# Block 2's four joints: the order of its small mixers, the rooms of the S5 and RG-LRU rows, of the first feed-forward sums and of the raw places

## The chip, the cores and the metric

The kernel runs on one NeuronCore of a Trainium2 chip, in one launch. A core has five engines with their own instruction queues: TensorE (PE; PEld is its weight load), VectorE (DVE), ScalarE (ACT), GpSimd (POOL) and SyncE (SP), which here only issues transfers. Transfers run on 16 DMA engines; SP, ACT and POOL issue them, and a "q" behind an engine's name in the profile is its queue. SBUF is the working memory, PSUM takes what TensorE computes, DRAM tensors carry what doesn't fit. The metric is the device time of one execution in microseconds (us), as the median of several runs.

## The reference

Two transformer blocks run one after the other over 1024 rows of 1024 numbers in fp32: a first one with attention and a mixture of experts, and a second one, cut here to what the change touches.

```python
def second_block(x, ...):
    h = rmsnorm(x, attn_norm[l])
    q, k, v, g, gk_low, s5_u, rg_x, rg_gate = jnp.split(h @ w_in[l], splits, axis=-1)
    y_gla = gla_mixer(q, k, v, g, gk_low, gla_w_gk_up[l], gla_b_gk[l], gla_norm[l])
    y_s5 = rmsnorm(s5_mixer(s5_u, ...), s5_norm[l])
    y_rg = rmsnorm(rglru_mixer(rg_x, rg_gate, ...), rg_norm[l])
    x = x + jnp.concatenate([y_gla, y_s5, y_rg], axis=-1) @ w_out[l]
    h = rmsnorm(x, mlp_norm[l])
    x = x + conv_ffn(h, w_up[l], mlp_conv_w[l], mlp_conv_b[l], w_down[l])
    return rmsnorm(x, final_norm)

def rglru_mixer(xr, gate, ...):
    xc = causal_dwconv(xr, conv_w, conv_b)
    r = jax.nn.sigmoid(jnp.einsum('blhi,hij->blhj', xh, w_a).reshape(B, L, RG_WIDTH) + b_a)
    i = jax.nn.sigmoid(jnp.einsum('blhi,hij->blhj', xh, w_x).reshape(B, L, RG_WIDTH) + b_x)
    log_a = -RG_C * r.astype(f32) * jax.nn.softplus(-lam.astype(f32))
    a = jnp.exp(log_a)
    xin = jnp.sqrt(-jnp.expm1(2.0 * log_a)) * (i * xc).astype(f32)
    _, h = lax.associative_scan(linear_rec_combine, (a, xin), axis=1)
    return h.astype(xr.dtype) * jax.nn.gelu(gate)

def s5_mixer(u, ...):
    ...
    y = jax.nn.gelu(y)
    y = y * jax.nn.sigmoid(y @ w_glu + b_glu)

def conv_ffn(h, w_up, conv_w, conv_b, w_down):
    up, gv = jnp.split(h @ w_up, 2, axis=-1)
    up = causal_dwconv(up, conv_w, conv_b)
    return (jax.nn.gelu(up) * gv) @ w_down
```

The sigmoids are computed as tanh of half the argument, and 1 + tanh is folded into the products that follow.

## The kernel before

Every large product is made of two parts of each factor: a cast to a rounded fp32 form (names with h or hi) and the rest (l or lo); three matmuls of 128x512 take the place of one (lines 260 to 262). The casts are mostly ScalarE's, the subtractions that give the rest VectorE's or GpSimd's. Weights come through a pool of raw tiles (wraw) and of hi and lo tiles (whi, wlo), which is also the room that the change takes for other things.

The second block passes through these stages; each is written once in Python, and a scheduler of the Tile layer sets the order of the instructions on each engine, the waits and the places of the tiles. Pools are opened and closed as stacks: a tile of a new pool lies where an earlier one was, and waits for its last users.

`mix_small` computes S5's input and its states by a scan over the rows (`s5_scan`, VectorE and GpSimd), RG-LRU's convolution (`rg_input`: xc), the two gates' matmuls (prg) with their tanh, the chain of exp, tanh and square root on ScalarE and products and a scan on VectorE, and stores the result, yS[2 + i]. Then comes the S5 output: sixteen groups of three matmuls (py), for which GpSimd copies the factors F (lines 1547 to 1550), VectorE evicts (line 1555), ScalarE applies the activation and issues 32 stores to y_d (line 1558). Then GLA's low-rank part (`gla_low`: pgl, gl), its decays (`gla_decays`: pgk, gz, ge, a scan to gb) and its projections (`gla_qk`: pp, qo), with S5's gate (pglu) between.

`gla_out` runs GLA in eight quads of two turns each (`quad`: decays gx, scores sc, kv, po, the transposes pty and the copies go), and puts the output projection between them. `rest(j)` is the S5 and RG-LRU half of the projection of 128 rows: it loads the raw rows from yS, casts them (YH), subtracts (YL), squares and sums for the norm (pr), makes four products and adds them to x, which it stores to x3_d. `last(j)` adds GLA's half, normalises the rows, and `cols` transposes them (pt) and makes from them the operands of the feed-forward part: 11, 21, 22 and the four differences T1 to T4 of a block product that takes seven half-size products for eight.

The feed-forward part (`Up`) has 22 features. Each loads two weight tiles (wr), makes four block sums on GpSimd (`sums` and `sum4`: fS and in place), casts and splits them (`weights`: wh, wl) and makes seven products (pa, pb, pc). For feature 0 only weights(0, 0) is made ahead; `first` makes its products with 11 and 21, and `first_out`, after the output work pool (ow, "o2work") has closed, makes its sums and other weights:

```python
        s_ow.close()
        self.F.rooms(self.pool(self.fws, "fw2"))
        self.F.first_out()
```

`ffn_down` multiplies the activations (act_d, stored by SP and GpSimd) by the down weights, 77 units of 128x1024 loaded as wraw from act_d and from the weights; `piece` loads a sixteenth of the residual x (res) with every second unit.

The functions that the change touches stand here with the lines of the profile.

Of the kernel before, what the change touches and what calls it, by code (L numbers as in the profile page):

```python
# [186 lines left out]
class K:  # L187
# [1232 lines left out]
    def mix_small(self, ps, st, XH, XL):  # L1420
# [74 lines left out]
        wr = rg.tile([128, 2, 2, 128], F32, name="rgw")  # L1495
        nc.sync.dma_start(wr, a["rg_w"])
        G = []
        for i in range(2):
            G.append([rg.tile([128, 1024], F32, tag=f"rgg{m}", name="rgg", bufs=2) for m in range(2)])
            for m in range(2):  # L1500
                for n in range(2):
                    c = slice(512 * n, 512 * n + 512)
                    pz = ps.tile([128, 512], F32, tag="mm", name="prg", bufs=2)
                    nc.tensor.matmul(pz, wr[:, m, i], xc[i][:, c], start=True, stop=True)
                    nc.scalar.activation(G[i][m][:, c], pz, AF.Tanh, bias=hba[:, m, i:i + 1], scale=0.5)


        for i in range(2):
            t, g = G[i]
            V.scalar_tensor_tensor(xc[i], g, 1.0, xc[i], op0=OP.add, op1=OP.mult)  # L1510
            nc.scalar.activation(g, t, AF.Exp, bias=p2[:, i:i + 1], scale=p2[:, i:i + 1])
        for i in range(2):
            t = G[i][0]
            nc.scalar.activation(t, t, AF.Tanh, bias=p[:, i:i + 1], scale=p[:, i:i + 1])
        for i in range(2):
            t, h = G[i][0], XR[i][:, 0:1024]
            nc.scalar.activation(h, t, AF.Sqrt, scale=0.25)
        for i in range(2):
            t, g = G[i]
            h = XR[i][:, 0:1024]  # L1520
            V.scalar_tensor_tensor(h, g, 1.0, h, op0=OP.add, op1=OP.mult)
            V.tensor_tensor(xc[i], xc[i], h, op=OP.mult)
            V.scalar_tensor_tensor(t, g, 1.0, t, op0=OP.add, op1=OP.mult)
            V.tensor_scalar(t, t, -1.0, 1.0, op0=OP.mult, op1=OP.add)
            V.tensor_tensor_scan(out=h, data0=t, data1=xc[i], initial=0.0, op0=OP.mult, op1=OP.add)
            V.tensor_tensor(xc[i], h, GT[i], op=OP.mult)
            nc.gpsimd.dma_start(self.yS[2 + i], xc[i])

# [32 lines left out]
        self.gla_decays(ps, qk, 0, gl, gu, gb, cm)  # L1561
        for t in range(2):
            self.gla_qk(ps, qk, XH, XL, 0, t)
# [129 lines left out]
    def gla_out(self, ps, lw, ms, XH, XL):  # L1693
# [128 lines left out]
        def rest(j):  # L1822

            c = slice(128 * j, 128 * j + 128)
            raw = ow.tile([128, 4, 128], F32, tag="yr", name="yr", bufs=4)
# [3 lines left out]
            YH, YL = yhl()  # L1829
# [29 lines left out]
        def last(j):  # L1859
# [11 lines left out]
            self.norm_rows(x, gm, xn, s)  # L1871
            if j:
                cols(X.pop(), j - 1)
# [8 lines left out]
        def cols(xn, j):  # L1882
# [81 lines left out]
        self.F.rooms(self.pool(self.fws, "fw2"))  # L1964
# [143 lines left out]
class Up:  # L2108
# [4 lines left out]
    def __init__(self, k):  # L2113
        self.k, self.nc, self.a, self.early, self.wk = k, k.nc, k.a, k.fw, None
        self.R, self.W, self.U, self.A, self.n = {}, {}, {}, {}, {}

    def ring(self, tag, of, dtype=F32):

        n = self.n[tag] = self.n.get(tag, -1) + 1
        first = tag == "wr" and n % of < 2 or n % of == 0  # L2120
        return (self.early if first else self.wk).tile([128, 1024], dtype, tag=f"{tag}{n % of}", name=tag, bufs=1)

    def rooms(self, pool):

        self.wk = pool

        def place(tag, n, dtype=F32):
            self.wk.tile([128, 1024], dtype, tag=tag, name="place", bufs=n)
        for tag, n in (("gv", 2), ("ft", 2), ("fX", 2), ("wr2", 1), ("wr3", 1), ("fS", 1)):
            place(tag, n)  # L2130
        for i in range(1, 5):
            place(f"wh{i}", 1, F32R)
            place(f"wl{i}", 1, F32R)
        self.cv = self.wk.tile([128, 4, 22], F32, name="fcv")
        self.nc.sync.dma_start(self.cv, self.a["fconv"])
# [16 lines left out]
    def sums(self, i):  # L2152

        if i < 22:
            G, t0, t1 = self.nc.gpsimd, self.T0, self.T1
            ru, rv = self.R[i]
            s = self.R[i, "s"] = self.wk.tile([128, 1024], F32, tag="fS", name="fS", bufs=1)
# [27 lines left out]
    def gelu(self, i):  # L2185
# [3 lines left out]
        t = self.A[i] = self.wk.tile([128, 1024], F32, tag="ft", name="ft", bufs=2)  # L2189
# [5 lines left out]
    def pair(self):  # L2195
        return [self.wk.tile([128, 1024], F32, tag="fX", name="fX", bufs=2) for _ in range(2)]
# [130 lines left out]
```

## Time and profile before

| | us |
|---|---|
| median of 3 runs (lowest, highest) | 2086.76 (2086.03, 2090.46) |
| the profiled execution | 2082.21 |
| its span in the profile | 2079.9 |
| TensorE busy | 1919.3 (92%) |
| VectorE busy | 1319.6 (63%) |
| ScalarE busy | 931.4 (45%) |
| GpSimd busy | 721.9 (35%) |
| second block's part of the span, from 1137 on, TensorE's waits in it of over 8 us | 12.8, 10.6 and 8.4 |

The busy time of an engine is an average over stages, so the share of 92% says that most stages are TensorE's and not that all are. The rows further down are from the same profiled execution: a stretch that is cut out with each engine's busy time, the waits of an engine with what released it, and timelines, in which a row may stand for several instructions in a row (x8) and the bracket tells how long the engine had been idle and what it had waited for. Names are those of the program without their buffer numbers.

### The profile page before, as it was taken

The numbers are of one execution on the slowest core, as the hardware profiler recorded it, in microseconds if no ns is written. First come the engines' busy times: TensorE is split into PE (matmuls) and PEld (weight loads), VectorE is DVE, ScalarE is ACT, GpSimd is POOL, SyncE is SP. The second block draws the span as 40 slices with busy tenths as digits, with TensorE's granted clock in tenths as the row PEclk, the third lists the DMA queues.
The fourth block names the chain that finished last, engine by engine and source line by source line (L and its number), as shares of the span: only waits on it lengthen the run. The fifth ranks groups of instructions, "written<-read, shape, count | busy, mean of one in ns | idle before, by whom it ended". The sixth has DMA issues, their size and how long they took to land.

```text
span 2079.9 us, 27638 instructions
## 1 busy us (share of the span) xinstructions
PE 1919.3 (92%) x9481; PEld 1515.4 (73%) x9481; DVE 1319.6 (63%) x2668; ACT 931.4 (45%) x1647; POOL 721.9 (35%) x721
## 2 busy tenths in 40 slices
PE   7999999999899699995999979996999999979998
PEld 6878777776678576764887657775888888868886
DVE  4156667565657677766458566878767666645565
ACT  4255555444433377764422563454333333324344
POOL 2111102343442111105435234216678677630130
PEclk9999999999999799997999999998999999989999
DMA  6153322333432799966524265553444444358664
GB/s 242 60 134 96 94 71 79 99 90 102 142 114 77 241 316 313 314 237 218 175 82 75 83 206 195 176 206 127 143 168 156 146 177 151 118 195 295 194 193 170
DMA packets 162148, 336.42 MB, mean 162 GB/s; under 512 B 26352, under 2 KB 71696, under 8 KB 161488
## 3 DMA queue, kind: packets, MB, share of 16 engines
q1 hardware_dynamic: 140448, 264.84, 38.7%
q0 software_dynamic: 18848, 68.43, 9.9%
q10 hardware_dynamic: 2704, 1.31, 0.3%
q8 instruction: 77, 1.26, 0.3%
q14 instruction: 71, 0.58, 0.1%
HBM read 237.98 MB, written 87.03 MB: 156 GB/s over the span
## 4 chain that ended last, share of the span: by engine, by line
PE 39%; DVE 6%; DMA 3%; ACT 2%; issue 2%; POOL 1%; ACTq 0%; SPq 0%; POOLq 0%; DVEq 0%
PE pd L260 3%; PE pd L261 3%; PE pd L262 3%; PE pb L262 3%; PE pb L260 3%; PE pb L261 3%; PE pc L260 2%; PE pc L262 2%; PE pc L261 2%; PE pa L261 2%; PE pa L260 2%; PE pa L262 2%; PE pvg L262 1%; PE pvg L260 1%; PE pvg L261 1%
## 5 line engine op out<-in xcount | busy, mean ns | idle before, releaser
L237 ACT CAST whi<-wraw 128x1024 fp32r<-128x1024 f32 x122 | 127.8, 1049 | 134.3 <-PE pp L261 63.8
L260 PE MATMUL pp<-XH,whi 128*128 128x512 f32 x416 | 167.4, 402 | 0.9 <-DVE kk L404 0.9
L262 PE MATMUL pp<-XH,wlo 128*128 128x512 f32 x416 | 165.8, 399 | 0.0
L261 PE MATMUL pp<-XL,whi 128*128 128x512 f32 x416 | 165.4, 398 | 0.0
L238 DVE TENSOR_TENSOR wlo<-wraw,whi 128x1024 fp32r<-128x1024 f32 x96 | 117.3, 1223 | 57.7 <-ACT whi L237 56.4
L1994 DVE TENSOR_TENSOR wlo<-wraw,whi 128x1024 fp32r<-128x1024 f32 x71 | 89.9, 1266 | 79.2 <-ACT whi L1993 74.4
L260 PE MATMUL pd<-whi 128*128 128x512 f32 x308 | 121.0, 394 | 12.9 <-ACT whi L1993 12.9
L2149 ACT CAST wh<-wr 128x1024 fp32r<-128x1024 f32 (+1 forms) x66 | 59.9, 910 | 158.8 <-PE pc L261 46.2
L238 POOL TENSOR_TENSOR wlo<-wraw,whi 128x1024 fp32r<-128x1024 f32 x26 | 63.5, 2444 | 174.0 <-ACT whi L237 157.6
L1993 ACT CAST whi<-wraw 128x1024 fp32r<-128x1024 f32 x71 | 74.8, 1054 | 106.2 <-PE pd L262 81.1
L261 PE MATMUL pd<-wlo,whi 128*128 128x512 f32 x308 | 121.3, 394 | 0.8 <-DVE wlo L1994 0.8
L262 PE MATMUL pd<-whi,wlo 128*128 128x512 f32 x308 | 120.8, 392 | 0.0
L1059 POOL DMA_INDIRECT xg<-xn_d,idx x25 | 30.0, 1198 | 188.3 <-PE pt L278 146.7
L260 PEld LDWEIGHTS pp<-XH,whi 128*128 128x128 f32 x416 | 79.0, 190 | 17.9 <-PE pp L262 1.7
L262 PEld LDWEIGHTS pp<-XH,wlo 128*128 128x128 f32 x416 | 78.7, 189 | 16.7 <-issue 2.2
L261 PEld LDWEIGHTS pp<-XL,whi 128*128 128x128 f32 x416 | 78.7, 189 | 15.1 <-issue 1.5
L2150 DVE TENSOR_TENSOR wl<-wr,wh 128x1024 fp32r<-128x1024 f32 (+1 forms) x66 | 83.6, 1268 | 8.1 <-ACT wh L2149 8.1
L531 ACT ACTIVATE PP<-PP,stat 128x256 f32<-128x256 f32 x128 | 64.5, 504 | 36.2 <-DVE stat L529 34.1
L260 PEld LDWEIGHTS pd<-whi 128*128 128x128 f32 x308 | 58.2, 189 | 26.8 <-ACT whi L1993 14.2
L2053 POOL TENSOR_TENSOR res<-res,p 128x512 f32<-128x512 f32 x12 | 23.8, 2010 | 134.5 <-DVE res L2051 134.5
L261 PEld LDWEIGHTS pd<-wlo,whi 128*128 128x128 f32 x308 | 58.4, 189 | 14.4 <-DVE wlo L1994 2.1
L529 DVE CUSTOM_DVE_ANT_0 PP<-sp,bias 128x256 f32<-128x256 f32 x128 | 52.9, 422 | 24.7 <-PE sp L527 19.3
(708 smaller groups left out, 5809.9 us busy)
## 6 DMA issues: line engine op xcount, KB each, us to landing
wraw<-in_wgu_dram SPq DMA_DIRECT2D x64, 512.0 KB
wr<-in_wup_dram SPq DMA_DIRECT2D x44, 512.0 KB
wraw<-act_d SPq DMA_DIRECT2D x77, 256.0 KB
wraw<-in_wdn_dram SPq DMA_DIRECT2D x32, 512.0 KB
fX<-in_wdown_dram SPq DMA_DIRECT2D x22, 512.0 KB
wdt_d<-fX SPq DMA_DIRECT2D x44, 256.0 KB
wraw<-wdt_d SPq DMA_DIRECT2D x44, 256.0 KB
O<-ot SPq DMA_DIRECT2D x17, 512.0 KB
```

The costliest lines, as they stand in the source:

```text
L237: nc.scalar.copy(hi, raw)
L238: (eng or nc.vector).tensor_tensor(lo, raw, hi.bitcast(F32), op=OP.subtract)
L260: nc.tensor.matmul(out, lh, rh, start=start, stop=False, **kw)
L261: nc.tensor.matmul(out, lh, rl, start=False, stop=False, **kw)
L262: nc.tensor.matmul(out, ll, rh, start=False, stop=stop, **kw)
L529: nc.vector.tensor_tensor_reduce(out=PP[j // 4][:, j % 4], in0=so, in1=bs, op0=OP.add, op1=OP.min, scale=1.0, scalar=3e38, accum_out=nm)
L531: nc.scalar.activation(PP[j // 4][:, j % 4], PP[j // 4][:, j % 4], AF.Exp, bias=nm, scale=-1.0, accum_out=stt[:, stj[0], 1, stj[1]:stj[1] ...
L1059: nc.gpsimd.indirect_dma_start(out=xg[0:n], out_offset=None, in_=self.xn_d, in_offset=bass.IndirectOffsetOnAxis(ap=idx[0:n, s, p:p + 1], a ...
L1993: nc.scalar.copy(h[:, 0:n], src)
L1994: nc.vector.tensor_tensor(l[:, 0:n], src, h[:, 0:n].bitcast(F32), op=OP.subtract)
L2149: self.nc.scalar.copy(h[:, 0:w], src)
L2150: self.nc.vector.tensor_tensor(l[:, 0:w], src, h[:, 0:w].bitcast(F32), op=OP.subtract)
```

## The change

1. In `mix_small` the block of RG-LRU's gates, from the load of rg_w to the stores of yS[2 + i], moves behind the S5 output, `gla_low` and the first `gla_decays`. The accumulators of prg alternate between the tags "a" and "mm"; before, all were "mm".
2. `rest(j)` takes its raw rows and YH, YL in one "whi" and one "wlo" tile of the weight pool, of which there are two each, in place of tiles of the work pool: four for the raw rows, two each for YH and YL.
3. The output weights wout2b get a stack of their own above the work pool. In `last(7)` it is closed as soon as those rows are normalised, and `weight_rooms` puts fS and the places 1 to 3 of wh and wl there; `first_weights` makes the sums and the other weights of feature 0 at this point, ahead of the last two `cols`, and no longer in `first_out`.
4. `cols` splits T2 as soon as it is there, then T3, T1, T4, and 22 last; before, 22 came first.
5. `ffn_down` places 5 whi, 4 wraw and 5 wlo tiles in the weight pool before its work pool is opened.

```diff
@@ mix_small
-        wr = rg.tile([128, 2, 2, 128], F32, name="rgw")
...
         gl, gu, gb, cm = self.gla_low(ps, qk, XH, XL)
         self.gla_decays(ps, qk, 0, gl, gu, gb, cm)
+
+        wr = rg.tile([128, 2, 2, 128], F32, name="rgw")
+        nc.sync.dma_start(wr, a["rg_w"])
...
+                    pz = ps.tile([128, 512], F32, tag="am"[m] + "m" * m, name="prg", bufs=2)
+                    nc.tensor.matmul(pz, wr[:, m, i], xc[i][:, c], start=True, stop=True)
+                    nc.scalar.activation(G[i][m][:, c], pz, AF.Tanh, bias=hba[:, m, i:i + 1], scale=0.5)
...
+            nc.gpsimd.dma_start(self.yS[2 + i], xc[i])
         for t in range(2):
             self.gla_qk(ps, qk, XH, XL, 0, t)
@@ rest
-            raw = ow.tile([128, 4, 128], F32, tag="yr", name="yr", bufs=4)
+            h, l = (self.wp.tile([128, 1024], F32R, tag="w" + x, name="w" + x, bufs=self.nhl) for x in ("hi", "lo"))
+            YH, YL, raw = (t.rearrange("p (k t) -> p k t", k=4) for t in (h[:, 0:512], h[:, 512:], l[:, 0:512].bitcast(F32)))
             nc.sync.dma_start(raw, self.yS[:, :, c].rearrange("k p t -> p k t"))
             x = ow.tile([128, 1024], F32, tag="x", name="x", bufs=2)
             nc.sync.dma_start(x, self.x2_d[c])
-            YH, YL = yhl()
@@ last
             self.norm_rows(x, gm, xn, s)
+            if j == 7:
+                s_wb.close()
+                self.F.weight_rooms(self.pool(self.fws, "fw2"))
+                self.F.first_weights()
             if j:
                 cols(X.pop(), j - 1)
@@ cols
             V.tensor_tensor(t[1], p22, t[0], op=OP.subtract)
+            split("T2", t[1])
             V.tensor_tensor(t[2], p22, t[3], op=OP.subtract)
+            nc.gpsimd.tensor_tensor(t[3], b21, t[1], op=OP.subtract)
+            split("T3", t[2])
+            split("T1", t[0])
+            split("T4", t[3])
             split("22", p22)
-            nc.gpsimd.tensor_tensor(t[3], b21, t[1], op=OP.subtract)
-            for i in (1, 2, 0, 3):
-                split(f"T{i + 1}", t[i])
@@ gla_out
-        s_ow = ExitStack()
-        wb = self.pool(s_ow, "wout2b", side="right")
+        s_ow, s_wb = ExitStack(), ExitStack()
+        ow = self.pool(s_ow, "o2work", side="right")
+        wb = self.pool(s_wb, "wout2b", side="right")
...
-        ow = self.pool(s_ow, "o2work", side="right")
@@ ffn_down
+        for tag, n, dtype in (("whi", 5, F32R), ("wraw", 4, F32), ("wlo", 5, F32R)):
+            self.wp.tile([128, 1024], dtype, tag=tag, name="place", bufs=n)
         wk = self.pool(st, "dwork")
@@ Up
+    def weight_rooms(self, pool):
+
+        self.pools["fS"] = pool
+        self.place("fS", 1)
+        for i in range(1, 4):
+            for t in ("wh", "wl"):
+                self.pools[f"{t}{i}"] = pool
+                self.place(f"{t}{i}", 1, F32R)
...
+    def first_weights(self):
+        self.sums(0)
+        self.sum4(0)
+        for n in range(1, 4):
+            self.weights(0, n)
```

Three places show what the scheduler made of it. The first is ScalarE in the gate block, from the activations of RG-LRU's gate (GT) on: before, the tanh of the gates (rgg from prg) with the exp, and square root passes (L1511, L1514, L1517), and after them the S5 output's activation (y) and stores (y_d).

```order
L1493 ACTIVATE GT<-pp 128x512
L1505 ACTIVATE rgg<-prg,rgsp 128x512 x6
L1511 ACT_TABLE_LOAD
L1511 ACTIVATE rgg<-rgg,rgsp 128x1024
L1505 ACTIVATE rgg<-prg,rgsp 128x512 x2
L1514 ACTIVATE rgg<-rgg,rgsp 128x1024
L1517 ACT_TABLE_LOAD
L1517 ACTIVATE XR<-rgg 128x1024
```

Now the same engine from the same row on, where gl is the copy of GLA's low-rank rows, and gz and ge are its decays:

```order
L1493 ACTIVATE GT<-pp 128x512
L1522 ACTIVATE y_13625<-y_13625 128x512
L1524 DMA y_d<-y_13625 16x4x128 x8
L1522 ACTIVATE y_13660<-y_13660 128x512
L1524 DMA y_d<-y_13660 16x4x128 x8
L1522 ACTIVATE y_13695<-y_13695 128x512
L1650 COPY gl<-pgl 48x512
L1524 DMA y_d<-y_13695 16x4x128 x8
L1522 ACTIVATE y_13730<-y_13730 128x512
L1650 COPY gl<-pgl 48x512
L1524 DMA y_d<-y_13730 16x4x128 x8
L1670 ACTIVATE gz<-pgk,gkb 128x512 x2
```

All 32 store issues now stand ahead of the first tanh of a gate, which comes in the row behind these.

The second place is SP at the turn from the first quads to the S5 rows. Before, the raw rows (yr from yS) come after the second go store (yG) and its quad's loads:

```order
L1722 DMA gq<-qk_d 128x3x256 x2
L1810 DMA wgr_14075<-in_wout_dram 128x1024
L1810 DMA wgr_14077<-in_wout_dram 128x1024
L1810 DMA wgr_14079<-in_wout_dram 128x1024
L1810 DMA wgr_14081<-in_wout_dram 128x1024
L1804 DMA yG<-go 128x2x128
L1758 DMA v<-v_d 128x256
L1760 DMA sg<-sg_d 128x256
L1758 DMA v<-v_d 128x256
L1760 DMA sg<-sg_d 128x256
L1722 DMA gq<-qk_d 128x3x256
```

In the changed program the first of them (wlo from yS) stands between the two gq loads, ahead of the output weights wgr:

```order
L1722 DMA gq<-qk_d 128x3x256
L1827 DMA wlo<-yS 128x4x128
L1722 DMA gq<-qk_d 128x3x256
L1810 DMA wgr_14075<-in_wout_dram 128x1024
L1810 DMA wgr_14077<-in_wout_dram 128x1024
L1810 DMA wgr_14079<-in_wout_dram 128x1024
L1810 DMA wgr_14081<-in_wout_dram 128x1024
L1804 DMA yG<-go 128x2x128
```

The first raw load is thus some dozen rows earlier, and one quad's gq and the four wgr loads stand behind it.

The third place is SP at the entry of the down projection. Before, behind the last stores of the activations (act_d from ft), loads of units alternate with one residual load (res) for two units:

```order
L2204 DMA act_d<-ft 128x512
L2218 DMA act_d<-ft 128x512
L2219 DMA act_d<-ft 128x512
L2024 DMA wraw<-act_d 128x512
L2025 DMA wraw<-in_wdown_dram 128x512
L2024 DMA wraw<-act_d 128x512
L2025 DMA wraw<-in_wdown_dram 128x512
L2016 DMA res_19140<-x_d 128x512
```

Now:

```order
L2222 DMA act_d<-ft 128x512
L2025 DMA res_19139<-x_d 128x512 x3
L2236 DMA act_d<-ft 128x512
L2237 DMA act_d<-ft 128x512
L2025 DMA res_19139<-x_d 128x512 x7
L2033 DMA wraw<-act_d 128x512
L2034 DMA wraw<-in_wdown_dram 128x512
```

Ten of the sixteen residual loads have moved ahead of the first unit, seven of them behind the last activation store. The first cast of that stage on ScalarE, in the changed program, waits for fifteen semaphores, among them those of GpSimd's last stores from fX; before, it waited for the two loads of its unit.

## Rows read from the trace of the kernel before

**Rows 1.** PE, PEld, DVE, ACT, POOL busy by stretch, granted clock, DMA share, GB/s.

```profile
1137.00:1162.00 25.00, 21.34 (x118) 14.86 (x117) 17.71 (x21) 17.17 (x20) 14.08 (x22) 0.93 0.13 43
...
1237.00:1256.00 19.00, 4.86 (x14) 2.93 (x14) 9.29 (x22) 11.19 (x27) 4.95 (x7) 0.71 0.76 255
1256.00:1330.00 74.00, 71.71 (x378) 57.14 (x377) 57.25 (x136) 23.13 (x76) 28.41 (x44) 0.98 0.55 180
...
1395.00:1425.00 30.00, 12.66 (x55) 9.37 (x55) 28.66 (x37) 16.00 (x27) 13.94 (x10) 0.73 0.34 124
...
1863.00:1870.00 7.00, 7.00 (x32) 5.74 (x31) 3.23 (x3) 3.57 (x4) 0.00 (x0) 1.00 1.04 403
```

**Rows 2.** Waits of TensorE, 1100 to 1900: us in total, times, longest.

```profile
PE pd L260 <- ACT whi L1993: 12.8, 1, 12.8
PE pb L260 <- ACT wh L2149: 10.6, 1, 10.6
PE po L260 <- ACT yh L1830: 8.4, 1, 8.4
```

**Rows 3.** Timeline of TensorE, gate block: start, us, engine, line, operation, count.

```profile
1145.89 5.55 PE L1504 MATMUL prg<-xc,rgw 128*128 128x512 f32 x8 [3.57 <-DVE xc L1467]
...
1161.64 0.48 PE L1648 MATMUL pgl<-XH,gkw 128*48 128x512 f32 x1
...
1170.24 0.50 PE L260 MATMUL pp<-XH,whi 128*128 128x512 f32 x1
```

**Rows 4.** Timeline of ScalarE, gate block and store issues.

```profile
1142.36 0.69 ACT L1505 ACTIVATE rgg<-prg,rgsp 128x512 f32<-128x512 f32 x1 [0.36 <-PE prg L1504]
...
1168.31 3.65 ACTq L1558 DMA_DIRECT2D y_d<-y  x8
1174.26 0.63 ACT L1556 ACTIVATE y<-y 128x512 f32<-128x512 f32 x1 [5.52 <-DVE y L1555]
...
1185.42 1.06 ACT L1672 ACTIVATE ge<-gz 128x1024 f32<-128x1024 f32 x1
...
1186.98 1.28 ACT L1673 ACT_TABLE_LOAD   x1
```

**Rows 5.** Timeline of GpSimd: copies that feed the S5 output.

```profile
1152.03 9.32 POOL L1547 COPY F<-s5F 64x128 f32<-64x128 f32 x18 [8.77 <-PE py L1550]
```

**Rows 6.** Timeline of all engines, S5 and RG-LRU rows.

```profile
1239.41 0.69 DVE L1687 COPY qo<-pp 128x512 f32<-128x512 f32 x1
...
1242.10 0.60 SPq L1826 DMA_DIRECT2D yr<-yS  x1
...
1247.44 0.62 ACT L1830 CAST yh<-yr 128x512 fp32r<-128x512 f32 x1 [1.20 <-DMA yr<-yS]
...
1258.03 0.77 PE L1842 MATMUL pr<-ones,yr 128*128 128x1 f32 x4
```

**Rows 7.** Timeline of all engines, before the feed-forward part.

```profile
1395.54 1.21 DVE L2150 TENSOR_TENSOR wl<-wr,wh 128x1024 fp32r<-128x1024 f32 x1
...
1415.30 0.68 DVE L1896 TENSOR_TENSOR XT1l<-xt,XT1h 128x512 fp32r<-128x512 f32 x1
...
1415.90 1.75 DVE L1896 TENSOR_TENSOR XT2l<-xt,XT2h 128x512 fp32r<-128x512 f32 x1
...
1418.86 1.59 POOL L2159 TENSOR_TENSOR fS<-fS,wr 128x512 f32<-128x512 f32 x1
1419.25 1.75 DVE L1896 TENSOR_TENSOR XT4l<-xt,XT4h 128x512 fp32r<-128x512 f32 x1
...
1422.62 0.80 PE L260 MATMUL pb<-XT2h,wh 128*128 128x512 f32 x1 [10.62 <-ACT wh L2149]
```

**Rows 8.** Timeline of all engines, entry of the down projection.

```profile
1852.36 0.42 SPq L2219 DMA_DIRECT2D act_d<-ft  x1
...
1856.45 1.04 ACT L1993 CAST whi<-wraw 128x1024 fp32r<-128x1024 f32 x1 [5.75 <-DMA wraw<-in_wdown_dram]
...
1858.20 0.56 POOL L2224 DMA_DIRECT2D act_d<-fX  x1
```

More of the change, by code (lines that the diff above doesn't have):

```diff
@@ L1493, in mix_small @@
                 nc.scalar.activation(GT[i][:, 512 * n:512 * n + 512], pp, AF.Gelu_apprx_tanh)
-        wr = rg.tile([128, 2, 2, 128], F32, name="rgw")
[L1496 to L1527, printed above, removed]
         dcol = s5.tile([128, 16], F32, name="dcol")
@@ L1561, in mix_small @@
         self.gla_decays(ps, qk, 0, gl, gu, gb, cm)
+        wr = rg.tile([128, 2, 2, 128], F32, name="rgw")
+        nc.sync.dma_start(wr, a["rg_w"])
+        G = []
+        for i in range(2):
+            G.append([rg.tile([128, 1024], F32, tag=f"rgg{m}", name="rgg", bufs=2) for m in range(2)])
+            for m in range(2):
+                for n in range(2):
+                    c = slice(512 * n, 512 * n + 512)
+                    pz = ps.tile([128, 512], F32, tag="am"[m] + "m" * m, name="prg", bufs=2)
+                    nc.tensor.matmul(pz, wr[:, m, i], xc[i][:, c], start=True, stop=True)
+                    nc.scalar.activation(G[i][m][:, c], pz, AF.Tanh, bias=hba[:, m, i:i + 1], scale=0.5)
+        for i in range(2):
+            t, g = G[i]
+            V.scalar_tensor_tensor(xc[i], g, 1.0, xc[i], op0=OP.add, op1=OP.mult)
+            nc.scalar.activation(g, t, AF.Exp, bias=p2[:, i:i + 1], scale=p2[:, i:i + 1])
+        for i in range(2):
+            t = G[i][0]
+            nc.scalar.activation(t, t, AF.Tanh, bias=p[:, i:i + 1], scale=p[:, i:i + 1])
+        for i in range(2):
+            t, h = G[i][0], XR[i][:, 0:1024]
+            nc.scalar.activation(h, t, AF.Sqrt, scale=0.25)
+        for i in range(2):
+            t, g = G[i]
+            h = XR[i][:, 0:1024]
+            V.scalar_tensor_tensor(h, g, 1.0, h, op0=OP.add, op1=OP.mult)
+            V.tensor_tensor(xc[i], xc[i], h, op=OP.mult)
+            V.scalar_tensor_tensor(t, g, 1.0, t, op0=OP.add, op1=OP.mult)
+            V.tensor_scalar(t, t, -1.0, 1.0, op0=OP.mult, op1=OP.add)
+            V.tensor_tensor_scan(out=h, data0=t, data1=xc[i], initial=0.0, op0=OP.mult, op1=OP.add)
+            V.tensor_tensor(xc[i], h, GT[i], op=OP.mult)
+            nc.gpsimd.dma_start(self.yS[2 + i], xc[i])
         for t in range(2):
@@ L1963, in gla_out @@
         s_ow.close()
-        self.F.rooms(self.pool(self.fws, "fw2"))
+        self.F.rooms(self.pool(self.fws, "fw3"))
         self.F.first_out()
@@ L2119, in ring, with place, tile @@
         n = self.n[tag] = self.n.get(tag, -1) + 1
-        first = tag == "wr" and n % of < 2 or n % of == 0
-        return (self.early if first else self.wk).tile([128, 1024], dtype, tag=f"{tag}{n % of}", name=tag, bufs=1)
-    def rooms(self, pool):
[L2125 to L2134, printed above, removed]
-        self.nc.sync.dma_start(self.cv, self.a["fconv"])
+        return self.tile(f"{tag}{n % of}", 1, dtype)
+    def place(self, tag, n, dtype=F32):
+        self.pools[tag].tile([128, 1024], dtype, tag=tag, name="place", bufs=n)
+    def weight_rooms(self, pool):
[5 more added lines that the diff above has]
+                self.place(f"{t}{i}", 1, F32R)
+    def rooms(self, pool):
+        self.cv = pool.tile([128, 4, 22], F32, name="fcv")
+        self.nc.sync.dma_start(self.cv, self.a["fconv"])
+        for tag, n, dtype in (("gv", 2, F32), ("ft", 2, F32), ("fX", 2, F32), ("wr2", 1, F32), ("wr3", 1, F32),
+                              ("wh4", 1, F32R), ("wl4", 1, F32R)):
+            self.pools[tag] = pool
+            self.place(tag, n, dtype)
+    def tile(self, tag, bufs=1, dtype=F32):
+        return self.pools.get(tag, self.early).tile([128, 1024], dtype, tag=tag, name=tag, bufs=bufs)
     def feat(self, i):
@@ L2195, in pair @@
     def pair(self):
-        return [self.wk.tile([128, 1024], F32, tag="fX", name="fX", bufs=2) for _ in range(2)]
+        return [self.tile("fX", 2) for _ in range(2)]
     def act(self, i):
@@ L2232, in unit @@
     def unit(self, i):
[L2233 removed]
+        self.U[i] = [self.tile(t, 2) for t in ("up", "gv")]
         return self.U[i]
@@ L2239, in first_out @@
         self.nc.vector.tensor_tensor(up[:, self.T0], self.P[1], gv[:, self.T0], op=OP.add)
-        self.sums(0)
-        self.sum4(0)
-        for n in range(1, 4):
-            self.weights(0, n)
         self.load(1)
```

7 lines of the change are left out of this document (3 added, 4 removed).

## The prediction

> **What bounds the kernel now.** I read three views. First the table of stretches [rows 1]: TensorE is busy 71.71 of 74 us between 1256 and 1330, so there it is the bound, and time saved ahead of it is kept. It is idle in four places, which I call joints: the gate block at 1137 to 1162 (21.34 busy of 25), the S5 rows at 1237 to 1256 (4.86 of 19, granted clock 0.71), the entry of the feed-forward part at 1395 to 1425 (12.66 of 30, while VectorE is busy 28.66), and the entry of the down projection. Then TensorE's waits [rows 2]: 8.4 us for the cast of S5 rows, 10.6 for the cast of feed-forward sums, 12.8 for the first cast of the down projection. Last the timelines of the joints [rows 3 to 8], beside the order of the new program, resolved to what each instruction waits for. The change touches all four joints, and its sum is made joint by joint, against the profiled execution's 2082.21 us (a span of 2079.9 and 2.3 around it). That run lies 4.55 below the median of the timed runs, 2086.76; I apply the difference to the median. A difference under 0.2% (4.2 us) can't be told from none here.
>
> **Gate block (mix_small).** Its eight prg matmuls, the tanh, exp and square-root passes and the scan move behind the S5 output and the first GLA decay. What goes: prg waits 3.57 us for the convolution and takes 5.55 from 1145.89, so the S5 output ends and pgl begins at 1161.64 only [rows 3]. In the new order py stands first. Its second half still needs VectorE to evict, which it does after the convolution (1145.9, the end of that wait), and GpSimd's copies, 0.52 each (18 in 9.32 [rows 5]); twenty of them from 1139, with a weight split between (taken as 2.4, twice VectorE's 1.21 for that shape [rows 7]), give 1152. So pgl starts some 9.5 us earlier.
>
> That lead is lost on ScalarE. Four groups of an activation and eight y_d stores, 0.63 + 3.65 each [rows 4], start when the first eviction is through, about 1146, and last to 1163; two gl copies and waits for store slots make it 1165.5. Only then come the two gz, seven of the eight tanh (0.69 each), three passes of 1.06 and three table loads of 1.28: 13.2 us, to about 1179. The projection behind them can't start before: its accumulator room is that of a gate matmul whose tanh is among these. Before, it started at 1170.24 [rows 3]. That is 8.8 later; 1.3 goes off because the second pgk is already done, and about 2.5 comes on because TensorE has done little since 1163 and restarts at the lower granted clock, as after the idle stretch of the S5 rows (0.71 [rows 1]): 10 us behind. Part is given back, since the quads that follow wait for ScalarE's and VectorE's second decay chain, not for TensorE; following it through pglu, gz and the scan I get the first quad 3.5 us later. I take **+3.5**, between -3 (ScalarE ahead of my walk, the 3.57 saved) and +10 (nothing given back).
>
> **S5 and RG-LRU rows (rest).** The raw rows move from the output work pool to whi/wlo tiles of the weight pool. The first load now stands in SP's queue ahead of a gq and the four wgr loads; it waits for TensorE's last use of a spent weight, which is ahead of the quads, some 20 us before the idle stretch begins, and for the store of RG-LRU, which by the walk above falls near 1205. So cast and split are done before TensorE leaves gla_qk, near 1237 [rows 1], where it used to wait 8.4 [rows 2]. What is late next: the second group needs the accumulator that the qo copy frees, 1240.1 (1239.41 + 0.69 [rows 6]); then ScalarE has the second cast queued ahead of go, for which pkd waits. The second load can be issued at about 1237.6 at the earliest, when gla_qk is through with the other set and a gq load has gone out; from issue to cast such a load took 5.3 (1242.10 to 1247.44 [rows 6]), so cast at 1243, go at 1243.9. The x load is queued behind the store of go, and lands about 1248; then the third group starts at 1248.7. Before, it started when pr was over, 1258.6 [rows 6]. That is 9.9, plus 1.7 for half a quad that is then done already, less 2 for new waits of the accumulators on evictions: **-9.5**. It can't exceed the stretch's whole idle time, 14.1; I bound it by -12 and by -5.5 (only the 8.4, less the new 1.9 for qo and 1 behind it). TensorE's bound up to 1330 [rows 1] keeps it.
>
> **Entry of the feed-forward part (pools, first_weights, split order).** Before, the first product (pb) waits until 1422.62 for sums and casts that start after the output work pool closes [rows 7]. Now four GpSimd sums, three casts and three low-part subtractions (1.21, 1.21 and about 0.68) are done ahead of the last two columns. But that is on VectorE, which has 1.3 us free in these 30 [rows 1]. pb then waits for XT2l of the last column. It ended at 1417.65 (1415.90 + 1.75 [rows 7]); X22l and one subtraction, 0.68 each, go behind it and 3.1 comes ahead: 1419.4. Further, a VectorE subtraction of two SBUF operands which starts while GpSimd works takes 1.75, otherwise 0.68 (XT4l behind fS, XT1l [rows 7]). With up to four more such holds of 1.07 it is 1423.7. I take 1421.6: **-1**, between -3.2 and +2.5. The next loads (wr2, wr3) are later too, but needed only for the next feature.
>
> The Trainium skill (SBUF — State Buffer, section "SBUF: two separate sides") calls this pair of ports an exclusive lock, held for the whole instruction by whichever engine comes first. The trace agrees (1.75 against 0.68), and the rule speaks against putting sums beside a saturated VectorE; without it this joint would be -3.2.
>
> **Entry of the down projection (places, raw places moved).** Two things stand in the way of its first cast. In SP's queue, which used to issue the first wraw right behind the last act_d store (1852.36 [rows 8]), seven residual loads now come between (three more are ahead of the stores, in idle time). Each is 128 x 512 in fp32, 0.262 MB; seven are 1.84 MB, at the 403 GB/s of a saturated stretch [rows 1] 4.6 us, or 2.9 by issue time alone (0.42 each). And the first cast's place now lies where GpSimd's fX tiles were: the order shows it waiting for GpSimd's last act_d store, issued at 1858.20 for 0.56 [rows 8], so landed hardly before 1861. The cast was at 1856.45. Both give 1861 to 1862.5. The 12.8 us wait grows by **+5.5**, between +4 and +8; after it nothing is short of data, as TensorE had no idle time there before either.
>
> The Trainium skill (DMA: Bandwidth & Descriptors, section "Queues, rings and completion order") says that each DMA engine goes round the queue rows that have work, packet by packet. By that GpSimd's store isn't held behind SP's seven loads, but the wraw loads on SP's own row are: the rule alone would give about +4.6. No row here shows the arbitration.
>
> **Sum.** +3.5 - 9.5 - 1 + 5.5 = -1.5, so 2080.7 for a profiled execution and **2085.3** on the scale of the median.
>
> **Rivals.**
> - *The gate block costs nothing* (chance 0.32). If ScalarE gets through its stores faster, or the quads give back all, only the saved wait stays: -3 - 9.5 - 1 + 5.5 = -8, 2078.8. For it: the second decay chain ended that stretch, not TensorE. Against: 32 store issues of 0.46 have nowhere else to go.
> - *The gate block's delay carries through* (0.18): the same chain, nothing given back, +10 - 9.5 - 1 + 5.5 = +5, 2091.8, slower. It decides as soon as the gate block's loss is above 9.2, which is the restart at 1179 with the lower clock and full GLA work behind. For it: the tanh and table loads that sit between the stores and the projection; against: the 14.1 us of idle time later, in which a late TensorE loses less.
> - *The rows don't come earlier* (0.06): the first raw load holds SP's queue, because the RG-LRU store lands after 1220, and the wgr loads behind it are late as well. Then the joint gives -2 at most: +6, 2092.8. I see 15 us of room.
>
> **How the numbers follow.** My forecast, no measurable change, has 0.44: its joints' errors (3, 2.5, 2 and 1.5) leave about 5 around -1.5, and its own range is 2080.5 to 2090.5. Together: faster 0.33 (the first rival and the forecast's edge), same 0.43, slower 0.24. The range that leaves out 2 in 10 reaches from the first rival to the slower ones: 2078.5 to 2093.
>
> **What would show it.** Right: pgl near 1152 and the projection behind prg not before 1176; no wait of 8.4 at the first S5 group and the third group 5 to 11 us nearer to the last gla_qk; pb's wait now put down to XT2l; pd's wait about 18 us, put down to a GpSimd store or wraw. Wrong: a projection that starts before 1172, a pd wait of 13 or less, or a feed-forward entry more than 4 us shorter.

## The result and the profile after

The changed kernel takes 2098.68 us (median of 5 runs, 2097.59 to 2099.36) against 2087.26 for the kernel before on the same chip (5 runs): a ratio of 1.0052 with a 95% interval of 1.0037 to 1.0066. It is 11 us slower; I had forecast 1.5 us faster. The profiled execution took 2097.59 us with a span of 2095.7. On a second chip the ratio was 1.0060 (1.0039 to 1.0082).

The two profiled executions also differ where the program does not: pz, the first matmul of S5's states, which both reach by the same instructions, starts at 1100.08 before and at 1105.79 after, and over all runs between 1097.3 and 1107.5. So from here on a mark such as "118.2 behind pz" counts from that matmul. First the stretches that answer to [rows 1], moved by these 5.7 us (columns as there):

```profile
1142.70:1167.70 25.00, 22.08 (x134) 17.43 (x133) 14.59 (x22) 4.02 (x6) 13.20 (x22) 0.93 0.29 71
1242.70:1261.70 19.00, 15.10 (x65) 12.12 (x64) 12.79 (x30) 11.84 (x25) 5.42 (x8) 0.87 0.61 205
1261.70:1335.70 74.00, 68.09 (x363) 55.36 (x362) 62.34 (x143) 25.19 (x82) 27.12 (x44) 0.99 0.67 217
1400.70:1430.70 30.00, 14.09 (x56) 9.78 (x55) 27.04 (x35) 15.38 (x26) 15.44 (x11) 0.72 0.50 175
```

The idle stretch at the S5 rows has gone (15.10 busy of 19, 4.86 before). But the long stretch behind it, in which I had taken TensorE for the bound, is now busy for 68.09 of 74, not 71.71, and VectorE for 62.34, not 57.25. TensorE's waits, which answer to [rows 2]:

```profile
PE pd L260 <- ACT whi L1999: 23.0, 1, 23.0
PE pt L1894 <- DVE X22l L1900: 9.0, 3, 4.3
PE po L260 <- DVE x L1845: 5.1, 7, 1.5
PE prg L1538 <- ACT rgg L1539: 5.1, 2, 3.2
...
PE pb L260 <- ACT XT2h L1899: 1.4, 1, 1.4
PE pb L261 <- DVE XT2l L1900: 1.4, 1, 1.4
```

The 8.4 at the S5 rows and the 10.6 of pb are gone. In their places stand accumulators that wait for VectorE's x (5.1) and transposes that wait for X22l (9.0), and the wait of the down projection has grown from 12.8 to 23.0. The gate block, ScalarE first, which answers to [rows 4], then TensorE, to [rows 3]:

```profile
1154.82 4.84 ACTq L1524 DMA_DIRECT2D y_d<-y  x8
...
1169.77 3.65 ACTq L1524 DMA_DIRECT2D y_d<-y  x8
1173.46 1.27 ACT L1670 ACTIVATE gz<-pgk,gkb 128x512 f32<-128x512 f32 x2 [3.26 <-DMA y_d<-y]
...
1182.16 1.28 ACT L1539 ACT_TABLE_LOAD   x1
1183.45 2.42 ACT L1539 ACTIVATE rgg<-prg,rgsp 128x512 f32<-128x512 f32 x4
```

```profile
1161.20 0.47 PE L1648 MATMUL pgl<-XH,gkw 128*48 128x512 f32 x1
...
1184.19 2.08 PE L1538 MATMUL prg<-xc,rgw 128*128 128x512 f32 x2 [3.24 <-ACT rgg L1539]
1186.06 1.92 PE L1574 MATMUL pglu<-yf,wglu 128*128 128x512 f32 x2
1186.99 1.42 PE L260 MATMUL pp<-XH,whi 128*128 128x512 f32 x1
```

pgl comes 55.4 behind pz (61.6 before), but the projection pp only at 81.2 (70.2). Last the entry of the down projection, all engines, which answers to [rows 8]:

```profile
1858.84 0.43 SPq L2237 DMA_DIRECT2D act_d<-ft  x1
1859.31 3.35 SPq L2025 DMA_DIRECT2D res<-x_d  x7
...
1862.70 0.88 SPq L2033 DMA_DIRECT2D wraw<-act_d  x1
...
1863.63 0.67 SPq L2034 DMA_DIRECT2D wraw<-in_wdown_dram  x1
...
1864.68 0.56 POOL L2242 DMA_DIRECT2D act_d<-fX  x1
...
1873.19 2.01 ACT L1999 CAST whi<-wraw 128x1024 fp32r<-128x1024 f32 x2 [16.00 <-DMA wraw<-in_wdown_dram]
```

The first unit's loads are issued 3.4 us later than they could be, which I had reckoned; but the cast comes 9.6 us behind the second of them. That load lands 9.1 us behind its issue, near 1872.7, and GpSimd's last store 7.8 behind its own, near 1872.5.

### The profile page after: what moved, and what is told of

The parts are those of the page before. It is cut to its first block, busy times and chain, and to the rows that moved or that the text cites. A ratio compares the mean times of both kernels' runs of the same rounds, so it can differ in the third digit from the quotient of the medians.

```text
span 2095.7 us, 27617 instructions
## 1 busy us (share of the span) xinstructions
PE 1925.1 (92%) x9481; PEld 1520.8 (73%) x9481; DVE 1318.6 (63%) x2668; ACT 928.2 (44%) x1645; POOL 718.3 (34%) x721
```

## The experiments

Each ratio is to the kernel before on the same chip; the marks are us behind pz in one profiled execution: the first scores (sc), the third group of the S5 rows (the first product with wa2), the last product with wa3, the end of the feed-forward products (where pd's wait begins), and pd's wait.

| kernel | ratio (95%) | sc | 3rd group | last wa3 | wait begins | pd's wait |
|---|---|---|---|---|---|---|
| before | 1 | 118.2 | 158.6 | 221.9 | 744.7 | 12.8 |
| changed | 1.0052 (1.0037, 1.0066) | 126.2 | 158.0 | 221.2 | 745.5 | 23.0 |
| e1 gate block back | 1.0025 (1.0010, 1.0039) | 119.7 | 150.7 | 217.9 | 742.1 | 22.8 |
| e2 fX lower | 1.0059 (1.0037, 1.0080) | 125.8 | 156.9 | 220.0 | 743.6 | 22.2 |
| e3 residual held | 1.0040 (1.0023, 1.0056) | 127.9 | 159.4 | 222.5 | 746.4 | 21.9 |
| e4 both | 1.0003 (0.9988, 1.0018) | 123.7 | 154.7 | 217.8 | 741.6 | 12.8 |
| e5 e4, split back | 0.9998 (0.9985, 1.0011) | 124.0 | 156.7 | 219.8 | 743.4 | 13.1 |
| e6 e4, weights late | 1.0011 (0.9998, 1.0023) | 126.4 | 158.5 | 224.5 | 747.3 | 13.1 |
| e7 e4, gate block back | 0.9968 (0.9956, 0.9979) | 118.5 | 151.4 | 216.2 | 740.8 | 13.0 |
| e8 e4, stores by SP | 0.9983 (0.9969, 0.9997) | 125.2 | 157.3 | 224.4 | 748.3 | 13.0 |
| e9 rows only | 0.9985 (0.9975, 0.9996) | 117.5 | 148.4 | 215.4 | 740.5 | 12.9 |
| e10 e9, x in raw tiles | 0.9985 (0.9971, 0.9999) | 120.0 | 149.1 | 216.9 | 743.7 | 12.9 |
| e11 changed, no places | 1.0056 (1.0043, 1.0070) | 126.4 | 157.6 | 223.4 | 746.5 | 24.5 |
| e12 gate block only | 1.0033 (1.0020, 1.0046) | 123.4 | 162.2 | 225.6 | 749.0 | 13.1 |
| e13 e7, entry back | 0.9956 (0.9936, 0.9975) | 117.6 | 150.8 | 216.1 | 738.1 | 12.9 |
| e14 changed again | 1.0060 (1.0039, 1.0082) | 123.7 | 155.4 | 220.7 | 745.1 | 22.4 |
| e15 e7 again | 0.9965 (0.9952, 0.9977) | 117.5 | 150.4 | 213.8 | 737.0 | 13.1 |

The changed kernel, e2, e3, e4, e11 and e14 run the same instructions up to the down projection, and their marks there spread over 5 us. So a single pair of marks says little below 3 us, except pd's wait, which repeats to 0.7 in two executions of the changed kernel. Nor is the profiled execution always near the median: e7's took 2075.76 us, the least of its ten, e8's 2094.40, the most of its twelve.

**e1.** Part 1 is undone: the block stands ahead of dcol again, its accumulators all "mm".

> Part 1 undone: the gate block stands ahead of the S5 output again, all else as changed. My theory now (the gate block's 8 us, read between pgl's lead and the first sc, are carried to the end because TensorE is busy from 1256 on): 8 us less than the changed kernel, about 2090.5; the first sc and the last gla_qk come 7 to 9 us earlier, the down entry's wait stays near 23. Rival (the delay only fills time in which TensorE would wait for the S5 rows anyway): within 2 us of the changed kernel, about 2098, with the wait for the rows grown to 6 or more in its place.

6.5 us at sc and 3.4 at the end by its marks, 0.27% of the time: less than all, more than nothing. It fits neither as put; e7, e12 and e15 below bear on the size.

**e2, e3, e4.** The rooms of the feed-forward part in another order (e2), the residual loads held (e3), both (e4):

```diff
-        for tag, n, dtype in (("gv", 2, F32), ("ft", 2, F32), ("fX", 2, F32), ("wr2", 1, F32), ("wr3", 1, F32),
+        for tag, n, dtype in (("fX", 2, F32), ("ft", 2, F32), ("wr2", 1, F32), ("wr3", 1, F32), ("gv", 2, F32),
```

```diff
-        def piece():
+        def piece(h):
             if pieces:
                 j, c = pieces.pop(0)
+                V.tensor_copy(res[:, j, c][:, 0:1], h[:, 0:1].bitcast(F32))
...
-                    piece()
+                    piece(w[0])
```

> The rooms of the feed-forward part in another order, fX first and gv behind wr3, so that the first whi tile of the down projection no longer lies over fX; its first cast waits for its two loads alone. The ten residual loads stay ahead of the first unit. My theory (place and queue both cost, the queue order the smaller part, since wraw is issued at 1862.7 and 1863.6 and lands behind 1.84 MB of residual loads): 3 us less than the changed kernel, about 2095.5, pd's wait about 20. Rival A (the place over fX is all of it): 10 less, 2088.5, pd's wait near 13. Rival B (the residual loads are all of it): no change, pd's wait 23.

> Each residual load is held until the cast of its own unit is through (a one-column VectorE copy into its tile), so that none stands ahead of the first units; the first whi tile still lies over fX. My theory: the cast then waits for GpSimd's last store, issued at 1864.7 and landed near 1867.5: pd's wait 17 to 18, 5.5 us less than the changed kernel, about 2093. Rival A (the place is all of it): no change, pd's wait 22 to 23. Rival B (the residual loads are all of it): pd's wait near 13, 2088.5.

> Both edits of the two runs before it: fX's room lower and the residual loads held. My theory and rivals A and B alike: pd's wait back at about 13 and 10 us less than the changed kernel, about 2088.5. Rival C (the 10 us come from neither, but from the transfers of GpSimd's stores sharing the engines with the first loads, or from a later end of the activations): pd's wait 18 or more.

pd's wait is 22.2, 21.9 and 12.8. Either cause alone costs all but a microsecond of the 10, and only without both is it gone: they are not two terms of a sum but two chains of which the later counts, and both end at about the same time. The times agree: 1.0059, 1.0040 and 1.0003. In e2 it is the unit's load, 8.9 us from issue to cast, behind seven residual loads:

```profile
1851.07 3.65 SPq L2025 DMA_DIRECT2D res<-x_d  x7
...
1855.29 0.90 SPq L2034 DMA_DIRECT2D wraw<-in_wdown_dram  x1
...
1864.16 1.04 ACT L1999 CAST whi<-wraw 128x1024 fp32r<-128x1024 f32 x1 [15.21 <-DMA wraw<-in_wdown_dram]
```

In e3 the loads are early, four units of them, and the cast is released by GpSimd's store from fX, which was issued 7.4 us before:

```profile
1859.35 0.45 SPq L2035 DMA_DIRECT2D wraw<-in_wdown_dram  x1
...
1864.21 0.56 POOL L2243 DMA_DIRECT2D act_d<-fX  x1
1871.59 3.88 ACT L1999 CAST whi<-wraw 128x1024 fp32r<-128x1024 f32 x4 [14.86 <-DMA act_d<-fX]
```

In e4 the load takes 3.2 us from issue to cast, and the store no longer matters:

```profile
1849.75 0.45 SPq L2035 DMA_DIRECT2D wraw<-in_wdown_dram  x1
...
1852.95 1.04 ACT L1999 CAST whi<-wraw 128x1024 fp32r<-128x1024 f32 x1 [5.83 <-DMA wraw<-in_wdown_dram]
```

Rival C falls. Rival B came true in e2 and rival A in e3, which fits together only if either cause is enough; my sharing out of the 10 falls.

**e11.** Part 5 undone in the changed kernel (the loop of places is taken out).

> The changed kernel with part 5 undone. My theory (part 3 is what brings fX's room to the first place of the weight pool, and part 5 only puts whi there in place of the raw tiles): the first raw load itself then waits for GpSimd's last store, issued at 1864.7 in the changed kernel, so pd's wait is 23 to 27 and the time 0 to 4 us more than the changed kernel's, ratio 1.005 to 1.007. Rival, the prediction's own attribution (the placing is what costs): pd's wait near 13, 10 us less, ratio 1.0003.

As my theory had it: the wait is 24.5. Now the first raw load itself waits for the store, 6.5 us from its issue:

```profile
1865.08 0.56 POOL L2239 DMA_DIRECT2D act_d<-fX  x1
1871.62 0.32 SPq L2030 DMA_DIRECT2D wraw<-act_d  x1
...
1875.07 1.04 ACT L1999 CAST whi<-wraw 128x1024 fp32r<-128x1024 f32 x1 [17.48 <-DMA wraw<-in_wdown_dram]
```

So part 5 does not bring the collision; it takes 1.5 to 2 us off pd's wait by putting whi there and not wraw (no difference shows in the time). By exclusion it is part 3's rooms that put fX over the weight pool's first place: e9 and e12 have parts 2 and 1 alone and a wait of 13, and part 4 moves no room. The residual loads stand ahead of the units in this kernel too and in e2, but not in e9 or e12, so that order comes with part 3 or 4; I take it for the rooms' work, which no run shows. By what rule the scheduler makes it stays open.

**e5, e6, e13.** The entry of the feed-forward part, on e4 and on e7: `cols` splits 22 first again (e5), feature 0's sums and weights are made in `first_out` (e6), both (e13).

```diff
-            split("T2", t[1])
             V.tensor_tensor(t[2], p22, t[3], op=OP.subtract)
+            split("22", p22)
             nc.gpsimd.tensor_tensor(t[3], b21, t[1], op=OP.subtract)
...
+            for i in (1, 2, 0, 3):
+                split(f"T{i + 1}", t[i])
```

```diff
-                self.F.first_weights()
...
+        self.first_weights()
         self.load(1)
```

> On the version with fX's room lower and the residual loads held (its ratio to the kernel before was 1.0003): part 4 undone, so cols splits 22 first again. My theory: with 22 last, the accumulator of the second transposes is read by the last VectorE instruction of a column, and the next column's transposes wait for it (pt for X22l, 9.0 us in three waits in the changed kernel, 0.7 before). Undone, these waits fall to about 1, the last transposes come some 3.5 us earlier, XT2l stands 0.7 behind X22l, and the first pb comes 2.5 to 3.5 us earlier, counted from the transposes at 240 us behind pz: 3 us less, ratio about 0.999. Rival (the waits only fill time in which VectorE works through the same list, and T2 first pays 0.7): the first pb 0 to 1 us later, ratio 1.0005.

> On the same version: the sums and weights 1 to 3 of feature 0 are made in first_out again, behind the last column, in the rooms of the changed kernel. My theory (VectorE is the bound here, so three low parts of 1.21 ahead of the last column cost what they save, but the sums and casts of GpSimd and ScalarE are saved): the second pb product, and all behind it, 2 to 4 us later than in the version it stands on, ratio about 1.0015. Rival (making them ahead is a loss here, since they stand in VectorE's list before the splits that TensorE waits for): 1 to 3 us earlier, ratio 0.9995.

> The version with the gate block back, fX's room lower and the residual loads held (ratio 0.9968 to before), with parts 3's early weights and 4 undone: feature 0's sums and weights in first_out, 22 split first; the rooms stay those of the changed kernel. Theory by the marks in the profiles (the pd wait began 740.8 us behind pz with the two parts and 740.5 without them in the version with the rows alone): no difference, within 1.5 us of the run it stands on, ratio about 0.997. Rival by the medians (0.9968 against 0.9985 for the rows alone): 3.5 us more, ratio 0.9985.

My theory of e5 failed, and the rival holds. From the first pf (feature 0's products with 11 and 21) to the first pb it takes 22.9 us there and 24.6 in e4, but from the last wa3 to the first pf 76.0 against 74.3: what one place gains the other loses, and the transposes now wait for another entry of VectorE's list (xt, 9.4 in three waits). e6 is within the noise and decides nothing: from the last wa3 to the beginning of pd's wait it takes 522.8 against 523.8 in e4, and the intervals of the two ratios overlap. e13 and e15 ran side by side: from the last wa3 to the beginning of pd's wait 522.0 against 523.2, and the medians 2077.66 against 2080.08 have overlapping intervals. The early weights of part 3 and part 4 together gain nothing here; the 3.5 us that I had read from medians across chips were not there.

**e7, e12, e15.** The gate block's place, on e4 and on the kernel before.

> On the same version: part 1 undone. Theory from the first of these runs (there the first sc came 6.5 us earlier, counted from pz, but the last wa3 product only 3.3 earlier): the quads behind it give back about half, 2.5 to 3.5 us less at the end, ratio about 0.9988. Rival, my reading of the two traces alone (all of it carried): 8 us less, ratio 0.9965, the last wa3 product 6 to 8 us earlier.

> The kernel before with part 1 alone. Theory (part of the gate block's delay is kept, 4 us at the last wa3 product by the run with the gate block back): first sc near 125 us behind pz (118.2 before), last wa3 product near 226, ratio 1.002. Rival A (without part 2, the idle time at the S5 rows takes the delay up): last wa3 product at 222 to 223, ratio 1.0002. Rival B (all carried): 229, ratio 1.0035.

> The version with the gate block back, fX's room lower and the residual loads held, beside the one above that undoes the entry. By the marks 4 less than before, ratio 0.998; by its own earlier medians 0.9968; the pd wait near 13, beginning 740 to 742 us behind pz.

By the marks, pd's wait begins at 744.8 on average with the block behind (the six kernels named above) and at 740.0 with it ahead (e1, e7, e15): 4.8 us. At sc it is 7.0 (125.6 against 118.6). Alone on the kernel before, part 1 costs 4.3 by the marks (749.0 against 744.7) and 0.33% of the time, about 7 us with an interval from 4 to 10. The rival that had the delay taken up is out. The one that had it carried whole is not: by the marks the theory is nearer, but the medians are the rival's (0.9968 in e7, where it had 0.9965 and the theory's 0.9988 lies outside the interval; 1.0033 in e12, where it had 1.0035 and the theory 1.002). By the times the block costs 6 to 7 us, each known to 3 or 4: 0.27% between e1 and the changed kernel, 0.35% between e7 and e4, 0.33% in e12. That 4.8 is less than the 7.0 at sc speaks for some of it being given back, but the marks are too few to call it shown.

**e8.** The y_d stores of e4 are issued by `nc.sync`, not `nc.scalar`.

> On the same version: the gate block stays in its new place, and SP issues the 32 y_d stores in place of ScalarE. My theory (ScalarE's 32 issues of 0.46 us are what holds the gates' tanh and so the first projection): the projection behind prg starts 9 to 12 us earlier than in the version it stands on (68 to 71 us behind pz, not 79.7), the first sc 5 to 8 us earlier, and 2 to 4 us are left of it at the last wa3 product, ratio about 0.9985. Rival (GpSimd's copies, VectorE's evictions and the decay chain bind as much): the projection 3 us earlier at most, nothing at the end, ratio 1.0003.

The projection starts at 80.1, where e4 has 79.7: the theory failed. ScalarE is free of the issues, but VectorE's third eviction of y (there are two y tiles) waits for a store of y as long as before, 6.09 us in e8 and 6.38 in e4; gz comes only 2.0 earlier behind pz (65.0 against 67.0), and the gates' tanh still stand behind gz, ge and the table loads on ScalarE. VectorE in e8 and in e4, then ScalarE in e8:

```profile
1162.62 1.12 DVE L1521 SCALAR_TENSOR_TENSOR y<-U,dcol,py 128x128 f32<-128x128 f32 x4 [6.09 <-DMA y_d<-y]
```

```profile
1154.86 1.12 DVE L1521 SCALAR_TENSOR_TENSOR y<-U,dcol,py 128x128 f32<-128x128 f32 x4 [6.38 <-DMA y_d<-y]
```

```profile
1178.65 1.28 ACT L1674 ACT_TABLE_LOAD   x1
1179.95 1.06 ACT L1674 ACTIVATE ge<-ge 128x1024 f32<-128x1024 f32 x1
1181.02 1.28 ACT L1539 ACT_TABLE_LOAD   x1
1182.32 2.42 ACT L1539 ACTIVATE rgg<-prg,rgsp 128x512 f32<-128x512 f32 x4
```

The ratio, 0.9983, is nevertheless what the theory had forecast (0.9985). No mark explains it, and its interval overlaps with that of e4.

**e9, e10.** Part 2 alone on the kernel before, and then with x of these rows in the weight pool's raw tiles:

```diff
-            x = ow.tile([128, 1024], F32, tag="x", name="x", bufs=2)
+            x = self.wp.tile([128, 1024], F32, tag="wraw", name="x", bufs=self.nraw)
             nc.sync.dma_start(x, self.x2_d[c])
```

> The kernel before with part 2 alone (S5 and RG-LRU rows in whi and wlo tiles). Theory from the runs so far (the last wa3 product of the version with the gate block back came 216.2 us behind pz, against 221.9 before): 5 to 6 us less than before, ratio 0.9973; the wait of 8.4 is gone, and six waits of the accumulators for x, together 5 to 6 us, stand in its place. Rival (the size I predicted): 9.5 less, ratio 0.9954, with accumulator waits near 2.

> The run before it with one edit more: x of these rows lies in the spent raw tiles (four of them) and no longer in two tiles of the work pool. My theory (the third x load waits for the store of the first x, 1253.25 to 1258.85 in the version with the gate block back, and VectorE's eviction and the accumulator behind it): the accumulators' waits fall to 2 to 3, another 2 to 3 us less, ratio 0.996. Rival (these waits are VectorE's own queue, not the load): waits within 1 us of the run before it, the same time, ratio 0.9973.

In e9 the third group comes 10.1 us earlier, which is the predicted size (9.9), but at the last wa3 6.5 are left, near what the theory said, where pd's wait begins 4.2, and in the median 0.15% (3 us), less than either expected. The same matmuls from the third group to behind the last wa3, before and in e9 (columns as in [rows 1]; some matmul records are missing from either), and e9's wait for x (1.0 us before):

```profile
1258.70:1322.60 63.90, 61.73 (x324) 49.11 (x324) 48.70 (x114) 18.89 (x61) 24.98 (x37) 1.00 0.54 177
```

```profile
1255.80:1323.40 67.60, 61.97 (x317) 49.16 (x316) 53.89 (x119) 22.68 (x69) 23.77 (x36) 0.98 0.62 195
```

```profile
PE po L260 <- DVE x L1845: 3.6, 6, 1.1
```

TensorE's work is the same, but it is spread over 67.6 us and not 63.9: the accumulators wait for VectorE's evictions, and VectorE does 5.2 us more in it. More x tiles (e10) leave 4.7 us of these waits and the same time, so they are not the x loads'. Nor are they all VectorE's own work. An eviction multiplies by the row's norm factor r, which GpSimd makes from pr, and three of e9's five longer waits (2.1 of 3.4 us) stand before evictions for which VectorE itself sat idle until r was there; the longest, 1.11, ends with the first of these:

```profile
1281.50 1.61 DVE L1845 SCALAR_TENSOR_TENSOR x<-po,r,x 128x512 f32<-128x512 f32 x2 [0.81 <-POOL r L251]
```

The other two stand behind VectorE's other work. No run took either cause away.

## Why the prediction was wrong, step by step

**Entry of the down projection: +5.5 predicted, +10 measured.** Both mechanisms were named and both are there. The failed step is "Both give 1861 to 1862.5": I priced the residual loads by their bytes (2.9 to 4.6 us) and let the unit's loads land behind them as fast as alone, and I let the store land hardly 3 us after its issue. The load took 8.9 us to its cast (e2) and not 3.2 (e4), the store 7.4 (e3). The bound of +8 was too low for the same reason. In e2's 8.9 us the DMA engines were 0.98 busy, so there the load shares full engines; in e3's 7.4 us they were 0.75 busy, so sharing is not all of the store's time, and the rest stays open. That the store is slow is not the change's doing: in e9, which enters this stage as the kernel before does, GpSimd's 256 KB stores took 7.7 us to land, and no cast waited for them. That part 5 brings the wait was wrong as well: it came without part 5 too (e11). The Trainium skill (DMA: Bandwidth & Descriptors, section "Queues, rings and completion order") has each DMA engine go round the queue rows that have work. By that rule the prediction had a store that is not held behind another queue's loads, and +4.6; in e3 the store was nevertheless 7.4 us under way while SP's queue had four units of loads out. No run shows the arbitration itself.

**S5 rows: -9.5 predicted, about -4 kept.** The step to the third group was right: 9.9 predicted, 10.1 measured in e9. The 2 us put down for new waits on evictions were near as well (3.6 against 1.0 before). Nothing is seen of the 1.7 for half a quad done already: behind the third group TensorE has as much to do as before (61.97 against 61.73). The failed step is "TensorE's bound up to 1330 keeps it": of the 10.1 only 6.5 are left at the last wa3 and 4.2 where pd's wait begins. 71.71 busy of 74 was read as a bound; but VectorE, 57.25 busy, ran not far behind, and in e9 the stretch grew by 3.7 us, 2.6 of them waits for evictions, which were late in part by VectorE's other work and in part by GpSimd's r. What takes the rest is below what one pair of marks can tell.

**Gate block: +3.5 predicted, 4 to 5 by the marks, 6 to 7 by the times.** pgl came at 55.4 behind pz in place of 61.6 (6 earlier, 8 in e12 and e14; 9.5 predicted), the projection 11 later (9 in e12 and e14; 10 predicted), the first scores 7 later (3.5 predicted), the beginning of pd's wait 4.8. The mechanism held. What was mis-sized is what the quads give back: of the delay of the projection, 3 to 4 us and not 6.5 are gone by the first scores, and how much goes behind them is not settled. Why ScalarE is late was put down to its 32 store issues; e8 shows that their issue time alone does not decide, since with SP issuing them the projection is no earlier. Whether the landing of the stores or the chain of gz, ge, table loads and tanh does, no run separates.

**Entry of the feed-forward part: -1 predicted, 0 to +1 measured.** From the last wa3 to the beginning of pd's wait it takes 522.8 us before and 524.2 in the changed kernel, and with or without the entry's edits the runs differ by about as much (e5, e6, e13). pb's wait is put down to XT2l, as said, and to XT2h. Not foreseen were the transposes' waits for X22l, 9.0 us; with 22 split first again (e5) the transposes wait 12.6 for xt and X22l together, against 9.9 in the changed kernel, so VectorE's list as a whole is the likely limit.

**Sum.** +4.8 - 4.2 + 0 + 10 = +10.6, against the 10.9 of the ratio 1.0052 (of 2086.76). That they meet so closely is luck, since all but the last term are known to some 2 us only. The forecast's signs were right in three of four joints; by the marks 5.3 us were missed at the S5 rows and 4.5 at the down projection. Of the rivals, "the gate block's delay carries through" came nearest in its sign; but its sum has +5.5 for the down projection and -9.5 for the rows, the two terms that failed. The version that beats both kernels has the rows of part 2, the rooms of part 3 with fX lower, the residual loads held, and gate block and entry as before (e13): 0.9956 (0.9936 to 0.9975) of the time before, 8 to 9 us less. With the entry as changed it is 0.9968 and 0.9965 (e7, e15).

## What to carry to other kernels

A stretch with a busy share of 97% is not proof that time saved ahead of it is kept: add the work that is pushed into it to the next busiest engine, and see who evicts and what the evictions themselves wait for. Where two things delay one instruction, take each away alone and then both; here each alone cost nearly all of it, and taking away one would have acquitted it wrongly. When a pool's rooms are moved, look up which later tile comes to lie over which last user, in the next stage as well, and price a transfer by how long its like takes from issue to landing in the same stage, where a trace shows it, and not by its bytes or its own queue alone.

## What the runs showed of the hardware

Same instructions, different clock: e1 and e7 differ only in the rooms of the feed-forward part and in the residual loads, both behind this stretch, but in e1 the granted clock of TensorE was 0.83 in a stretch behind pz (160 to 180 us) in which e7 had 1.00, the level of 2.4 GHz, throughout; 78 matmuls were recorded there and not 94:

```profile
1259.10:1279.10 20.00, 17.51 (x78) 14.12 (x77) 14.37 (x29) 6.48 (x16) 7.62 (x12) 0.83 0.60 192
```

```profile
1257.30:1277.30 20.00, 17.73 (x94) 14.27 (x93) 16.73 (x33) 8.16 (x23) 9.00 (x13) 1.00 0.67 219
```

By the marks e1 takes 67.2 us from the third group to the last wa3 and e7 64.8, some 2.4 us more, as much as the terms under dispute, and why a joint was read here from several executions. Both had a 5 us piece of it with TensorE idle for a part (2.5 us in e1, 2.0 in e7); only in e1 did the granted clock fall, to 0.70 in that piece and 0.61 in the next 5 us, so partly to the level of 1.2 GHz. What decides it stays open.

A 256 KB load that takes 3.2 us from issue to its cast (e4) takes 8.9 when seven residual loads are ahead of it and GpSimd's stores beside it (e2), with the DMA engines 0.98 busy at 364 GB/s. GpSimd's 256 KB stores took 6.4 to 7.9 us from issue to landing in this stage (e11, e9 and the changed kernel).
